# Block sums from kept float32 tiles, and a written order of steps in place of a planner, in a one-core mixer layer

## The chip, the cores and the metric

The kernel runs on one NeuronCore of a Trainium2 chip. The metric is the time on the device, in microseconds (us). Five engines work from queues of their own and wait for each other by semaphores: TensorE (PE; its weight loads have rows of their own, PEld), VectorE (DVE), ScalarE (ACT), GpSimd (POOL), and SyncE (SP), which only issues DMAs.

## The reference

The reference is one pre-norm residual layer for 512 tokens of width 1024, in float32. A combined projection feeds two attention branches of eight heads each: A is latent attention with rotary keys, B keeps the best 128 keys of each query, scored by a small indexer, and adds a relative-position bias. Both are gated and projected, then weighted, summed, projected again, added to the input and normalised.

```python
h = rmsnorm(x, norm_g[l])
(q_lat, c_kv, k_rope, z_a, q_b, k_b, v_b, z_b,
 q_idx, k_idx, w_idx, gate_a, gate_b) = jnp.split(h @ w_in[l], cuts, axis=-1)
...
y_a = mla_attention(q_nope, q_pe, k_nope, k_pe, v_a, pos).reshape(B, S, MLA_WIDTH)
y_a = y_a * jax.nn.silu(z_a)
...
_, idx = lax.top_k(score, topk)
...
y_b = y_b * jax.nn.silu(z_b)
merged = (jax.nn.sigmoid(gate_a) * (y_a @ w_o_a[l])
          + jax.nn.sigmoid(gate_b) * (y_b @ w_o_b[l]))
x = x + merged @ w_out[l]
return rmsnorm(x, final_g)
```

## The kernel before, in words

**Numbers in two parts.** A float32 operand of a matmul is split into a rounded part ("hi", by a cast on ACT) and the remainder ("lo", value minus hi, on DVE or POOL), and a product is three matmuls: hi by hi, lo by hi, hi by lo. The input after normalisation lies transposed in eight tiles of 128 channels by 512 tokens. `normed(k)` (L845) makes tile k in float32 (a tile of class "tmp"), splits it into the pair `hT[k]` (tiles `s_h`), and gives the float32 tile back.

**Products with fewer multiplications.** Some of the projections use block sums: the tokens are halved (columns HI and LO), and the channels too (tile k and tile k+4), and sums and differences of these blocks are multiplied instead of all the blocks. `input_sums()` (L1090) makes these for the four pairs of tiles. For each pair it adds hi and lo again, into two new tiles (`s_tmp<-s_h,s_h`), makes four half-width sums on them in place (`s_tmp<-s_tmp` and `s_tmp<-s_tmp,s_tmp`, 256 columns), and splits the result into hi and lo (`s_hs`). It starts when `SUMS_AT = ("a", 5)` is done, head 5 of branch A. The products that read `s_hs` have sets of 256 columns, and their results meet in tiles `s_pair`, by a copy on ACT (L357) and an addition on DVE (L383).

**Weights.** A load (`raw<-w_...`, by SP, four buffers) is cast on ACT to `s_w` or `s_wo`; the low part is a subtraction on DVE (L383) or POOL (L385). Some weights also have block sums, `s_wsum`.

**Attention.** For each head and each of four tiles of 128 queries, branch A multiplies (L1664 to L1666), takes the row maximum on DVE (`TENSOR_REDUCE`, L1647), and the exponential on ACT. In branch B, ACT first copies the mask of the tile into a PSUM bank (`ps<-mask`, L357), PE adds the products (`ps<-s_op,qhi`), and DVE reads the bank with the bias (L1748). Then the probabilities are scaled by the reciprocal of their sum (`s_p<-s_p,sm`), turned by matmuls with the identity (L481), split (`s_ph`), and multiplied by the values (`ps<-s_ph,vv`).

**What sets the order.** The program is written as some 430 generators ("threads"), each of which yields steps, requests for buffers (`Get`) and conditions (`Until`). `Flow.run` (L224) keeps a model of the free time of each engine and buffer, and picks, each time, the step that would start first by that model. A step that can go to several engines goes where the model sees it end first. On top of the model lie numbers: `SETTLE` asks that PE's operands be ready 2 us before by the model, `NUDGE` adds a drawn number to each thread's rank, `FIRST` picks the second or third candidate at 47 places, `pbias` favours POOL or not, and `PASSED` holds four weight loads back behind 2 or 6 other loads. `Pool_.give` (L136) hands out the free buffer that was used longest ago. The result is one fixed instruction list for each engine. The program does not change it when it runs.

## Time and profile before

| | us |
|---|---|
| median of three runs (420.13 to 420.21) | 420.14 |
| the profiled execution, first to last instruction (its span) | 417.4 |
| PE busy, of the span | 410.4 (98%) |
| DVE busy | 372.8 (89%) |
| ACT busy | 297.9 (71%) |
| POOL busy | 125.7 (30%) |

The span is the profiled execution's own time; the runs are 2.7 us longer, and this part lies outside of the trace. A line of the profile is read so: program line, engine, operation, output tile <- input tiles, the shape, the count; then busy us and the mean in ns of one; then the idle time of that engine before these instructions and what ended it. "PE busy" counts modelled ends of overlapping matmuls, so it does not tell that PE runs at its best pace, only that it is nowhere without work.

### The profile page before, as it was taken

To read this page: it belongs to the slowest core of one execution; us is meant where nothing else is said; L and a number is where in the kernel's file an instruction comes from. 1 tells how busy PE (TensorE), PEld (TensorE's weight loads), DVE (VectorE), ACT (ScalarE), POOL (GpSimd) and SP (SyncE) were. 2 spreads that over 40 slices of the span, in tenths; PEclk is the share of its full clock that TensorE was granted. 3 is DMA by queue.
4 is the path that set the end of the run, shared out by engine and by line. 5 is a ranking of instruction groups with operands and counts; after the bars stand their busy time and mean duration, and the time that the engine had idled before them with its cause. 6 is when DMAs were issued, how large, how long until landed. Compare 5 with 4: busy or idle time off the path is not lost.

```text
span 417.4 us, 7522 instructions
## 1 busy us (share of the span) xinstructions
PE 410.4 (98%) x2494; PEld 370.5 (89%) x2494; DVE 372.8 (89%) x789; ACT 297.9 (71%) x688; POOL 125.7 (30%) x147
## 2 busy tenths in 40 slices
PE   8999999999999999999999999999999999999994
PEld 8999888888888888889999999999998888888883
DVE  4779889569999999999998999799889999999973
ACT  5776888575763846547649978998999975329753
POOL 0037769544464659610000410401001120021330
PEclk9999999999999999999999999999999999999999
DMA  7984135655256351553427336564249767377104
GB/s 266 359 291 143 51 93 190 182 172 136 100 134 188 97 166 40 139 140 110 143 53 204 111 127 175 143 150 149 93 113 296 249 184 240 107 263 264 50 26 176
DMA packets 30790, 65.90 MB, mean 158 GB/s; under 512 B 4792, under 2 KB 6472, under 8 KB 30752
## 3 DMA queue, kind: packets, MB, share of 16 engines
q1 hardware_dynamic: 28400, 61.79, 48.6%
q10 hardware_dynamic: 1584, 2.49, 1.7%
q0 software_dynamic: 768, 1.15, 0.9%
q8 instruction: 19, 0.31, 0.3%
q14 instruction: 19, 0.16, 0.1%
HBM read 50.49 MB, written 4.21 MB: 131 GB/s over the span
## 4 chain that ended last, share of the span: by engine, by line
PE 98%; DVE 0%; ACT 0%; DVEq 0%; issue 0%; ACTq 0%
PE ps L462 88%; PE ps L481 5%; PE ps L1665 1%; PE ps L1666 1%; PE ps L1664 1%; PE ps L957 1%; PE ps L611 1%; DVE s_rg L413 0%; ACT junk L366 0%; PE ps L1008 0%; DVEq L2322 0%; ACT sm L366 0%; DVE sm L2017 0%; DVE zeros L540 0%; DVE neghalf L540 0%
## 5 line engine op out<-in xcount | busy, mean ns | idle before, releaser
L462 PE MATMUL ps<-s_h,s_w 128*128 128x512 f32 (+1 forms) x672 | 135.8, 348 | 0.1
L462 PEld LDWEIGHTS ps<-s_h,s_w 128*128 128x128 f32 x672 | 106.8, 189 | 14.0 <-DVE s_pair L383 0.5
L357 ACT CAST s_w<-raw 128x512 fp32r<-128x512 f32 (+3 forms) x134 | 78.2, 595 | 16.1 <-DVE raw L383 12.1
L385 POOL TENSOR_TENSOR s_w<-raw,s_w 128x512 fp32r<-128x512 f32 (+2 forms) x42 | 52.1, 1253 | 61.5 <-ACT s_w L357 54.1
L383 DVE TENSOR_TENSOR s_w<-raw,s_w 128x512 fp32r<-128x512 f32 (+2 forms) x92 | 59.8, 663 | 9.7 <-ACT s_w L357 9.5
L462 PE MATMUL ps<-s_hs,s_w 128*128 128x256 f32 x384 | 51.9, 285 | 0.0
L462 PEld LDWEIGHTS ps<-s_hs,s_w 128*128 128x128 f32 x384 | 48.3, 191 | 0.1
L462 PE MATMUL ps<-s_ys,s_w 128*128 128x512 f32 x192 | 46.0, 392 | 0.0
L462 PEld LDWEIGHTS ps<-s_ys,s_w 128*128 128x128 f32 x192 | 35.7, 188 | 7.2
L462 PE MATMUL ps<-s_wo,s_mg 128*128 128x512 f32 (+1 forms) x156 | 33.7, 373 | 0.0
L462 PE MATMUL ps<-s_w,s_xg 128*128 128x328 f32 (+1 forms) x192 | 32.5, 323 | 0.0
L462 PEld LDWEIGHTS ps<-s_wo,s_mg 128*128 128x128 f32 x156 | 27.6, 188 | 5.2
L366 ACT ACTIVATE s_p<-s_p,sm 128x256 f32<-128x256 f32 (+3 forms) x58 | 31.0, 548 | 1.4 <-DVE sm L1748 1.3
L462 PEld LDWEIGHTS ps<-s_w,s_xg 128*128 128x128 f32 x192 | 31.4, 188 | 0.0
L357 ACT CAST s_ph<-ps 128x384 fp32r<-128x384 f32 (+1 forms) x48 | 23.6, 517 | 6.7 <-PE ps L481 5.7
L383 DVE TENSOR_TENSOR s_ph<-ps,s_ph 128x384 fp32r<-128x384 f32 (+1 forms) x48 | 27.2, 591 | 1.1 <-ACT s_ph L357 1.1
L366 ACT ACTIVATE s_p<-ps,sm 128x128 f32<-128x128 f32 (+3 forms) x32 | 16.8, 528 | 15.9 <-DVE sm L1647 15.8
L982 DVE MATCH_REPLACE8 mask<-sm,mask 128x384 f32<-128x384 f32 (+2 forms) x48 | 25.9, 542 | 0.0
L981 DVE MAX8 sm<-mask 128x8 f32<-128x384 f32 (+2 forms) x48 | 25.6, 548 | 0.1
L462 PE MATMUL ps<-s_ph,vv 128*128 128x512 f32 (+3 forms) x128 | 25.6, 319 | 0.0
L481 PE MATMUL ps<-ident,s_p 128*128 128x128 f32 x160 | 23.0, 273 | 0.0
L462 PEld LDWEIGHTS ps<-s_ph,vv 128*128 128x128 f32 x128 | 20.6, 189 | 2.0
(206 smaller groups left out, 783.4 us busy)
## 6 DMA issues: line engine op xcount, KB each, us to landing
raw<-w_out SPq DMA_DIRECT2D x18, 512.0 KB, 3.5
s_op<-s_op SPq DMA_DIRECT2D x36, 128.0 KB, 3.4
raw<-w_ga SPq DMA_DIRECT2D x8, 512.0 KB
raw<-w_gb SPq DMA_DIRECT2D x8, 512.0 KB, 3.6
raw<-w_o SPq DMA_DIRECT2D x16, 256.0 KB, 3.6
s_xn<-x SPq DMA_DIRECT2D x8, 256.0 KB, 5.2
bias_scratch<-s_sig ACTq DMA_DIRECT2D x8, 256.0 KB, 2.3
raw<-w_za SPq DMA_DIRECT2D x4, 512.0 KB, 4.5
```

Source lines behind the costliest of these rows:

```text
L357: nc.scalar.copy(dst.ap, src.ap)
L366: nc.scalar.activation(dst.ap, src.ap, func, **kw)
L383: opts.append(("DVE", 0.07 + 0.00104 * x.n, lambda: nc.vector.tensor_tensor(dst.ap, x.ap, y.ap, op=op)))
L385: opts.append(("POOL", 0.15 + 0.0021 * x.n, lambda: nc.gpsimd.tensor_tensor(dst.ap, x.ap, y.ap, op=op)))
L462: nc.tensor.matmul(ps.ap, l.ap, r.ap, start=start and i == 0, stop=stop and i == len(pairs) - 1, skip_group_check=more)
L481: nc.tensor.transpose(d.ap, s.ap, ident.tile)
L611: return lambda: nc.tensor.matmul(ps.tile[:, :n], z[:, :P], z[:, :n], start=True, stop=True)
L957: step = pe(0.005 + n / 2400, [ps.all], [qs[h].all, ks[0].all], lambda: nc.tensor.matmul(ps.tile[:, :n], qs[h].tile[:96, TOK[i]], ks[0].ti ...
L981: yield Step([("DVE", t, lambda: nc.vector.max(m8.tile, work.tile))], [m8], [work])
L982: yield Step([("DVE", t, lambda: nc.vector.match_replace(work.tile, m8.tile, work.tile, MARK))], [work], [m8])
L1664: nc.tensor.matmul(o, q0[0:100], k0[0:100], start=True, stop=False)
L1665: nc.tensor.matmul(o, q0[0:96], k1[0:96], start=False, stop=False)
```

## The change

Two things are changed. First, `normed` takes its float32 tile from a class of its own ("hx") and keeps it, and `input_sums` works on the kept tiles in place: the eight additions hi plus lo are gone, and the eight tiles are held from the normalisation to the sums. The sums may start when head 1 of branch A is done, `("a", 1)`. Second, `Flow.run` no longer decides. It walks a table, `ORDER`, of some 4,000 tokens: each names a thread (its number in base 62), after a dot the choice of engine where there are several, and after an equals sign the buffer that is granted. The model with its numbers is removed, `PASSED` is empty, and three places take their buffers or wait in a way that the table can name.

```diff
-    def give(self, req):
-        if not self.free or (req.cap is not None and self.used.get(req.cls, 0) >= req.cap):
-            return None
-        self.free.sort(key=lambda b: max(b.w, b.r))
-        fits = self.free
-        if req.adds is not None:
-            fits = [b for b in self.free if b.summed[0] <= req.adds[0] and b.summed[1] >= req.adds[1]]
-            if not fits:
-                return None
+    def give(self, req, name):
+        b, = (b for b in self.free if b.name == name)
+        assert req.cap is None or self.used.get(req.cls, 0) < req.cap
+        assert req.adds is None or (b.summed[0] <= req.adds[0] and b.summed[1] >= req.adds[1])
         self.used[req.cls] = self.used.get(req.cls, 0) + 1
-        b = fits[0]
         self.free.remove(b)
...
     def __init__(self):
-        self.free = {"PE": 0.6, "ACT": 0.6, "DVE": 0.6, "POOL": 0.6, "SP": 0.6}
-        self.hw, self.dma, self.adma = 0.6, 0.0, 0.0
-        self.pbias = -1.0
-        self.steps = 0
-        self.port = 0.0
-        self.threads = []
-
...
-    def spawn(self, gen, prio, nudge=None):
-        t = Thread(gen, prio, self.draw.random() * NUDGE if nudge is None else nudge)
+        self.threads, self.made = [], []
+
+    def spawn(self, gen, *rank):
+        t = Thread(gen)
+        self.made.append(t)
...
-    def run(self, stop=None):
-        while self.threads:
-            if stop and stop():
-                return
-            moved = False
-            for t in sorted(self.threads, key=lambda t: t.prio):
-                if isinstance(t.req, Get):
-                    b = t.req.pool.give(t.req)
-                    if b is not None:
-                        self.advance(t, b)
-                        moved = True
-                elif isinstance(t.req, Until) and t.req.cond():
+    def settle(self):
+        again = True
+        while again:
+            again = False
+            for t in list(self.threads):
+                if t.alive and isinstance(t.req, Until) and t.req.cond():
...
+    def run(self):
+        for token in ORDER.split():
+            self.settle()
+            name, _, buf = token.partition("=")
+            name, _, way = name.partition(".")
+            n = 0
+            for c in name:
+                n = 62 * n + DIGITS.index(c)
+            t = self.made[n]
+            step = t.req
+            if buf:
+                self.advance(t, step.pool.give(step, buf))
                 continue
-            best, ready = None, []
-            for t in self.threads:
-                if isinstance(t.req, Step):
-                    for i, (eng, dur, emit) in enumerate(t.req.options):
-                        s = self.start(t.req, eng)
-                        key = ((self.settled(t.req, eng, s) if eng in SETTLE and s < math.inf else s) + BIAS * t.prio + t.nudge, t.prio)
-                    if best is None or mine[5] < best[1][5]:
-                        best = (t, mine)
...
-            turn = FIRST.get(self.steps)
-            self.steps += 1
-            if turn:
-                same = sorted((x for x in ready if x[1][2] == best[1][2]), key=lambda x: x[1][5])
-                best = same[min(turn, len(same) - 1)]
-            t, (_, s, eng, dur, emit, _) = best
-            emit()
...
+            assert all(b.written or b in step.outs for b in step.ins)
+            step.options[int(way or 0)][2]()
             for b in step.outs:
-                b.w = max(b.w, end)
-                b.written, b.by = True, eng
+                b.written = True
...
-
-
-RAW_LAG = {"DVE": 0.125, "POOL": 0.1, "ACT": 0.1}
-BIAS = 0.01
-NUDGE = 0.01
-DRAW = 53
...
+
 PSQUARE = -50
-SETTLE = {'PE': {'DVE': 2.0, 'ACT': 2.0, 'POOL': 2.0, 'SP': 1.0}, 'SP': {'DVE': 1.0, 'ACT': 1.0, 'POOL': 1.0}}
...
-        flow.draw = random.Random(REDRAW)
-        flow.pbias = LATER
...
     def normed(k):
         yield Until(lambda: rbc and k in xg)
-        tmp = yield slot("tmp", TCAP)
+        tmp = yield slot("hx")
         yield stt(tmp.all.f, xt[k].all.f, normg[:, k : k + 1], rbc[0].all.f, ALU.mult, ALU.mult)
         put(xt[k])
         hi = yield slot("h")
         lo = yield slot("h")
         yield act(hi.all, tmp.all.f)
         yield lo_part(lo.all, tmp.all.f, hi.all)
-        put(tmp)
+        hx[k] = tmp
         hT[k] = (hi, lo)
...
     def input_sums():
 
-        yield Until(lambda: sums_due[0] in done)
+        yield Until(lambda: SUMS_AT in done or SUMS_AT is None)
         for k in range(4):
-            f = []
-            for i in (k, k + 4):
-                t = yield slot("tmp", TCAP)
-                yield soon(tt(t.all.f, hT[i][0].all.f, hT[i][1].all.f, ALU.add, BOTH))
-                f.append(t)
+            yield Until(lambda: k in hx and k + 4 in hx)
+            f = [hx[k], hx[k + 4]]
             x, y = (t.all.f for t in f)
             yield soon(tt(x[:, HI], x[:, LO], x[:, HI], ALU.subtract, BOTH))
             yield soon(tt(y[:, HI], y[:, HI], x[:, HI], ALU.subtract, BOTH))
...
         def at(self, i):
-            if self.buf is None:
-                self.buf = yield Get(SMALL)
             c = i - self.group[0]
             return self.buf[:, c : c + 1]
...
     def sums_of_head():
-        return {i: s for s in (Sums(g) for g in GROUPS) for i in s.group}
+        sums = [Sums(g) for g in GROUPS]
+        for s in sums:
+            s.buf = yield Get(SMALL)
+        return {i: s for s in sums for i in s.group}
...
-        ready, sums = set(), sums_of_head()
+        ready, sums = set(), (yield from sums_of_head())
...
         def partial(i):
+            yield Until(lambda: i in seven)
             u3 = seven[i].all.f
...
-ORDER = [0,1,2,3]
+TILES = (0, 1, 2, 3)
...
-FIRST = {
-    283: 2, 456: 1, 606: 1, 1070: 1, 1073: 1, 1078: 1, 1083: 1, 1157: 1, 1297: 1, 1302: 2, 1315: 2, 1328: 1,
...
-PASSED = {7: 2, 8: 2, 9: 2, 10: 6}
-SUMS_AT = ("a", 5)
+PASSED = {}
+SUMS_AT = ("a", 1)
...
+ORDER = (
+    "0=s0 1=s1 2=ps0 6=ps1 6=ps2 6=ps3 6=ps4 6=ps5 6=ps6 0 5=s2 5=s3 3 1 4=s4 4=s5 1 1=s6 1 1=s7 1 1=s8 1 1=s9 1 1=s10 1 1=s11 1 1=raw0 1 1=s12 0 0 0 1 "
...
```

The instructions are, with the exception of the eight additions, the same; their order and engine are not. PE has the same 2,494 matmuls, with the first 176 rows of its queue in the same order and about 1,460 of 2,509 rows in place over the whole. DVE has 721 rows where it had 738, POOL 160 where it had 152. Three places follow. A number behind a name is the tile's or bank's own, and differs between the two programs for the same thing; line numbers differ too.

**At the start of DVE's queue.** `s_er` is the first weight tile as loaded, `s_w_142` its hi part and `s_w_143` the lo part; `s_xg` is the lo part of the first input tile. Before:

```order
L733 TENSOR_SCALAR s_w_142<-s_er_139 128x256
L394 SCALAR_TENSOR_TENSOR s_xg_147<-s_x_140,normg,s_xg_146 128x256
L383 TENSOR_TENSOR s_w_143<-s_er_139,s_w_142 128x256
L394 SCALAR_TENSOR_TENSOR s_xg_147<-s_x_140,normg,s_xg_146 128x128 x2
L383 TENSOR_TENSOR s_w_226<-s_er_149,s_w_225 128x328
L394 SCALAR_TENSOR_TENSOR s_xg_230<-s_x_152,normg,s_xg_229 128x512
```

Now:

```order
L642 TENSOR_SCALAR s_w_142<-s_er_139 128x256
L294 TENSOR_TENSOR s_w_143<-s_er_139,s_w_142 128x256
L305 SCALAR_TENSOR_TENSOR s_xg_147<-s_x_140,normg,s_xg_146 128x256
L305 SCALAR_TENSOR_TENSOR s_xg_147<-s_x_140,normg,s_xg_146 128x128 x2
L294 TENSOR_TENSOR s_w_225<-s_er_149,s_w_224 128x328
L305 SCALAR_TENSOR_TENSOR s_xg_229<-s_x_151,normg,s_xg_228 128x512
```

The lo part of the weight has moved ahead of the 256-column piece of the input's lo part.

**The block sums.** POOL's queue where the first sums are made, before:

```order
L385 TENSOR_TENSOR s_w_1993<-raw_67,s_w_1992 128x512
L385 TENSOR_TENSOR s_tmp_2048<-s_h_615,s_h_616 128x512
L385 TENSOR_TENSOR s_tmp_2052<-s_h_695,s_h_696 128x512
L385 TENSOR_TENSOR s_tmp_2048<-s_tmp_2048 128x256
L385 TENSOR_TENSOR s_tmp_2052<-s_tmp_2052,s_tmp_2048 128x256
L385 TENSOR_TENSOR s_tmp_2048<-s_tmp_2052,s_tmp_2048 128x256
L385 TENSOR_TENSOR s_tmp_2052<-s_tmp_2052 128x256
```

DVE's queue where the second and third pair begin, before:

```order
L383 TENSOR_TENSOR s_hs_2178<-s_tmp_2052,s_hs_2177 128x512
L383 TENSOR_TENSOR s_ph_2096<-ps_99,s_ph_2095 128x512
L981 MAX sm_84<-mask_110 128x8
L982 MATCH_REPLACE mask_110<-sm_84,mask_110 128x256
L383 TENSOR_TENSOR s_tmp_2200<-s_h_681,s_h_682 128x512
L383 TENSOR_TENSOR s_tmp_2217<-s_h_645,s_h_646 128x512
L383 TENSOR_TENSOR s_tmp_2200<-s_tmp_2200 128x256
L383 TENSOR_TENSOR s_y_2232<-ps_95,s_tmp_2226 64x512
L383 TENSOR_TENSOR s_ph_2209<-ps_93,s_ph_2208 128x384
L383 TENSOR_TENSOR s_ph_2214<-ps_98,s_ph_2213 128x384
L981 MAX sm_81<-mask_110 128x8
L383 TENSOR_TENSOR s_tmp_2217<-s_tmp_2217 128x256
```

POOL's queue where the first pair is made, now (`s_hx_518` and `s_hx_522` are the kept float32 tiles):

```order
L296 TENSOR_TENSOR s_hx_518<-s_hx_518 128x256
L296 TENSOR_TENSOR s_w_1440<-raw_68,s_w_1439 128x256
L296 TENSOR_TENSOR s_hx_522<-s_hx_522,s_hx_518 128x256
L296 TENSOR_TENSOR s_y_1407<-s_y_1407,s_z_1188 128x512
L451 MEMSET mask_112 64x64
L296 TENSOR_TENSOR s_hx_518<-s_hx_522,s_hx_518 128x256
L296 TENSOR_TENSOR s_w_1464<-raw_69,s_w_1463 128x512
L296 TENSOR_TENSOR s_w_1503<-raw_69,s_w_1502 128x512
L296 TENSOR_TENSOR s_hs_1497<-s_hx_518,s_hs_1496 128x512
```

And DVE's queue at the same pair, now:

```order
L294 TENSOR_TENSOR s_hx_522<-s_hx_522 128x256
L892 MATCH_REPLACE mask_110<-sm_80,mask_110 128x256
L891 MAX sm_87<-mask_110 128x8
L1551 TENSOR_REDUCE sm_90<-ps_97 128x1
L1551 TENSOR_REDUCE sm_82<-ps_95 128x1
L891 MAX sm_81<-mask_112 128x8
L891 MAX sm_89<-mask_111 128x8
L1551 TENSOR_REDUCE sm_76<-ps_98 128x1
L1551 TENSOR_REDUCE sm_91<-ps_96 128x1
L1551 TENSOR_REDUCE sm_77<-ps_99 128x1
L305 SCALAR_TENSOR_TENSOR s_z_1492<-s_z_1492,ps_94 128x512
L1551 TENSOR_REDUCE sm_78<-ps_92 128x1
```

The additions of two `s_h` are gone, most half-width sums stand in POOL's queue, and the rest stands in DVE's queue between searches for the best keys (`MAX`, `MATCH_REPLACE`) and row maxima of branch A, where before it stood behind nearly all of these.

**ACT's queue in the last heads of branch B.** `ps<-mask` opens a tile of a head; `s_ys` are the hi parts of the gated outputs. Before:

```order
L366 ACTIVATE s_ys_4207<-s_y_2232 128x512
L366 ACTIVATE s_ys_4228<-s_y_4057 128x512
L366 ACTIVATE s_ys_4204<-s_y_1413 128x512
L366 ACTIVATE s_ys_4205<-s_y_1650 128x512
L366 ACTIVATE s_ys_4208<-s_y_3208 128x512
L357 CAST s_w_4172<-raw_67 128x512
L357 COPY ps_97<-mask_110 128x256
L366 ACTIVATE s_p_4115,sm_91<-s_p_4115,sm_85 128x384
L357 COPY ps_99<-mask_112 128x512
L366 ACTIVATE s_p_4181,sm_79<-s_p_4181,sm_89 128x128
L357 COPY ps_92<-mask_111 128x384
L366 ACTIVATE s_p_4202,sm_79<-s_p_4202,sm_82 128x256
```

Now:

```order
L277 ACTIVATE s_ys_4173<-s_y_3186 128x512
L268 COPY s_pair_3965<-ps_94 128x256
L277 ACTIVATE s_ys_4190<-s_y_4070 128x512
L268 CAST s_w_4193<-raw_68 128x512
L268 COPY ps_98<-mask_111 128x384
L268 COPY ps_99<-mask_110 128x256
L268 CAST s_w_4207<-raw_67 128x512
L277 ACTIVATE s_p_4122,sm_88<-s_p_4122,sm_85 128x128
L277 ACTIVATE s_p_4123,sm_88<-s_p_4123,sm_76 128x256
L277 ACTIVATE s_pair_3793<-s_pair_3793 128x512
L277 ACTIVATE s_p_4182,sm_89<-s_p_4182,sm_82 128x128
L268 COPY ps_95<-mask_112 128x512
```

PE's queue where it uses these banks, before (`qhi_72` and `qhi_73` belong to the two heads):

```order
L462 MATMUL ps_93<-s_h_636,s_w_4159 128x512
L462 MATMUL ps_97<-s_op_3236,qhi_73 128x256
L462 MATMUL ps_97<-s_op_3237,qhi_73 128x256
L462 MATMUL ps_93<-s_h_661,s_w_4145 128x512
L462 MATMUL ps_93<-s_h_662,s_w_4145 128x512
L462 MATMUL ps_93<-s_h_661,s_w_4159 128x512
L462 MATMUL ps_99<-s_op_3258,qhi_72 128x512
L462 MATMUL ps_99<-s_op_3384,qhi_72 128x512
L462 MATMUL ps_92<-s_op_3236,qhi_73 128x384
L462 MATMUL ps_92<-s_op_3237,qhi_73 128x384
```

Now:

```order
L373 MATMUL ps_96<-s_h_551,s_w_4194 128x512
L373 MATMUL ps_98<-s_op_3261,qhi_72 128x384
L373 MATMUL ps_98<-s_op_3472,qhi_72 128x384
L373 MATMUL ps_96<-s_h_580,s_w_4193 128x512
L373 MATMUL ps_96<-s_h_581,s_w_4193 128x512
L373 MATMUL ps_96<-s_h_580,s_w_4194 128x512
L373 MATMUL ps_95<-s_op_3261,qhi_72 128x512
L373 MATMUL ps_95<-s_op_3472,qhi_72 128x512
L373 MATMUL ps_96<-s_h_642,s_w_4193 128x512
L373 MATMUL ps_96<-s_h_643,s_w_4193 128x512
L373 MATMUL ps_96<-s_h_642,s_w_4194 128x512
```

Five `s_ys` pieces stood together ahead of three mask copies; now single `s_ys` pieces and casts stand between copies. In PE's queue three tiles of the two heads stood within ten rows; now two tiles of one head stand in eleven.

More of the change, by code (lines that the diff above doesn't have):

```diff
@@ L295, in run @@
             self.advance(t, None)
-RAW_LAG = {"DVE": 0.125, "POOL": 0.1, "ACT": 0.1}
-BIAS = 0.01
-NUDGE = 0.01
-DRAW = 53
+        self.settle()
+        assert not self.threads
 PSQUARE = -50
-SETTLE = {'PE': {'DVE': 2.0, 'ACT': 2.0, 'POOL': 2.0, 'SP': 1.0}, 'SP': {'DVE': 1.0, 'ACT': 1.0, 'POOL': 1.0}}
 TC_ARGS = {}
@@ L971, in scores @@
             put(*qs.values(), *ks)
+            done.add("scored")
         flow.spawn(topk(i), PTOPK)
@@ L1648, in soft @@
                 mx.tile[:, 1:2], ps.tile[:, :n], op=ALU.max, axis=AX.X, negate=True))], [mx], [ps])
-            den = yield from sums[i].at(i)
+            den = sums[i].at(i)
             yield act(probs[i], ps[:, :n], AF.Exp, bias=mx[:, 1:2], scale=1.0, accum=den)
@@ L1653, in soft @@
             ready.add(i)
-        for i in ORDER:
+        for i in TILES:
             nn = P * (i + 1)
@@ L1741, in dsa_head @@
         slots, probs = yield from prob_tiles("p", 6)
-        ready, biased, sums = set(), set(), sums_of_head()
+        ready, biased, sums = set(), set(), (yield from sums_of_head())
         def soft(i, ps):
@@ L1756, in soft @@
                 put(bias)
-            den = yield from sums[i].at(i)
+            den = sums[i].at(i)
             yield act(p, p, AF.Exp, bias=mx[:, 1:2], scale=-1.0, accum=den)
@@ L1762, in soft @@
             ready.add(i)
-        for i in ORDER:
+        for i in TILES:
             nn = P * (i + 1)
```

79 lines of the change are left out of this document (6 added, 73 removed), and 103 rows, old and new, of tables (FIRST, ORDER).

## The prediction

> **What bounds the kernel now.** I read the page first: the busy times and the chain that ended last.
>
> ```profile
> PE 410.4 (98%) x2494; PEld 370.5 (89%) x2494; DVE 372.8 (89%) x789; ACT 297.9 (71%) x688; POOL 125.7 (30%) x147
> ...
> PE 98%; DVE 0%; ACT 0%; DVEq 0%; issue 0%; ACTq 0%
> ```
>
> The chain is PE for 98% of the span. It is not a chain that hops between engines: PE's queue simply runs through. Then I asked for PE's waits. The view of waits (time, number, longest) has one real row for PE, at the start, and a few for its weight loads:
>
> ```profile
> PEld L611 <- DVE neghalf L540: 1.1, 1, 1.1
> PEld ps L462 <- DVE s_pair L383: 0.5, 2, 0.2
> PEld ps L462 <- ACT ps L357: 0.4, 1, 0.4
> ```
>
> The first is the start of the program, which stays. So PE waits for other engines for about 0.9 us after it has begun. The timeline shows where (start, us, engine, what, and in brackets the idle time before):
>
> ```profile
> 260.80 2.20 PEld L462 LDWEIGHTS ps<-s_h,s_w 128*128 128x128 f32 x18 [0.24 <-DVE s_pair L383]
> ...
> 299.81 0.77 PEld L462 LDWEIGHTS ps<-s_h,s_w 128*128 128x128 f32 x6 [0.24 <-DVE s_pair L383]
> ...
> 323.50 0.30 PEld L462 LDWEIGHTS ps<-s_op,qhi 128*128 128x128 f32 x2 [0.44 <-ACT ps L357]
> ```
>
> Whatever the new order does for the other engines, it can give back no more than these three, and a little at the start. What PE itself costs depends on the number of matmuls, which does not change, and on which shapes follow each other. From the chain's pieces in order of time (start, us, what):
>
> ```profile
> 56.73 0.44 PE ps L481 x4
> ...
> 77.71 6.14 PE ps L462 x27
> ```
>
> 27 matmuls of 512 columns take 6.14 us, 0.227 us each; four transposes 0.44 us, 0.11 each although they are 128 columns wide. Going over the pairs of neighbours in both lists of PE with such paces, I find PE's own work the same within 0.1 us (149 transposes follow a transpose before, 145 now). I take 0 for this.
>
> Then the stages, by windows (bounds: length, PE busy, PEld, DVE, ACT, POOL, clock, DMA share, GB/s):
>
> ```profile
> 0.00:100.00 100.00, 98.94 (x556) 89.77 (x557) 76.48 (x149) 73.67 (x169) 51.43 (x72) 1.00 0.61 192
> 100.00:180.00 80.00, 80.00 (x426) 68.63 (x425) 79.45 (x202) 47.87 (x116) 44.88 (x52) 1.00 0.44 122
> 180.00:320.00 140.00, 139.93 (x1077) 135.57 (x1076) 129.87 (x273) 115.20 (x274) 14.12 (x11) 1.00 0.49 138
> 320.00:400.00 80.00, 79.99 (x378) 66.64 (x378) 78.83 (x148) 53.28 (x108) 11.65 (x7) 1.00 0.57 194
> ```
>
> DVE is as full as PE from 100 to 180 us (79.45 of 80) and from 320 to 400 us, and yet PE has no wait there. DVE is behind in the sense that its queue is never empty, but it is ahead of what PE needs. Work taken off DVE is therefore hidden by PE; what counts is whether any single step now comes later than its matmul.
>
> **The change, part by part.**
>
> The sums. The prices by shape (count, busy us, mean ns):
>
> ```profile
> L383 DVE TENSOR_TENSOR s_tmp<-s_h,s_h 128x512 f32<-128x512 f32 x6 | 3.8, 680 | 0.0
> L385 POOL TENSOR_TENSOR s_tmp<-s_h,s_h 128x512 f32<-128x512 f32 x2 | 2.5, 1294 | 0.0
> L383 DVE TENSOR_TENSOR s_tmp<-s_tmp 128x256 f32<-128x256 f32 x5 | 2.1, 414 | 0.0
> L385 POOL TENSOR_TENSOR s_tmp<-s_tmp,s_tmp 128x256 f32<-128x256 f32 x4 | 3.0, 740 | 2.2 <-DVE s_tmp L383 2.0
> L385 POOL TENSOR_TENSOR s_tmp<-s_tmp 128x256 f32<-128x256 f32 x3 | 2.6, 852 | 3.4 <-DVE s_tmp L383 3.4
> L383 DVE TENSOR_TENSOR s_hs<-s_tmp,s_hs 128x512 fp32r<-128x512 f32 x7 | 4.7, 680 | 0.0
> ```
>
> and, from the timeline, the one low part on POOL:
>
> ```profile
> 168.96 1.31 POOL L385 TENSOR_TENSOR s_hs<-s_tmp,s_hs 128x512 fp32r<-128x512 f32 x1
> ```
>
> DVE loses six additions (6 x 0.68 = 4.1 us), six half-width steps that go to POOL (6 x 0.41 = 2.5) and four low parts (4 x 0.68 = 2.7), together 9.3 us. POOL loses two additions (2.6) and takes six half-width steps at about 0.8 (4.8) and four low parts (5.2): 7.4 us more, in a core where POOL is busy for 30%. On PE's path this is worth 0: the first matmul with `s_hs` is at the same place in PE's queue as before, the sums now start some 40 us ahead of it, and PE had no wait for them before. If that cover were gone, one pair of tiles on POOL would cost its chain, 4 x 0.8 + 1.3 = 4.5 us; it is about a tenth of the lead.
>
> The first instructions. The rows around PE's first real work:
>
> ```profile
> 4.18 0.48 DVE L394 SCALAR_TENSOR_TENSOR s_xg<-s_x,normg,s_xg 128x256 fp32r<-128x256 f32 x1 [0.51 <-ACT s_xg L366]
> 4.30 2.16 PE L462 MATMUL ps<-s_xg,s_w 128*128 128x256 f32 x8
> 4.58 0.42 DVE L383 TENSOR_TENSOR s_w<-s_er,s_w 128x256 fp32r<-128x256 f32 x1
> ```
>
> The weight's lo part stands behind a step that waits for ACT until 4.18; it ends at 5.0. In the new order it can run in DVE's idle 0.51 us before, and the step behind is later by at most 0.42. PE runs on through both. Between 0 and 0.42 us could be gained; since PE's row shows no gap that long, I take 0.1.
>
> The three waits. The one at 323.50 has a clear cause in ACT's queue:
>
> ```profile
> 316.55 0.63 ACT L366 ACTIVATE s_ys<-s_y 128x512 fp32r<-128x512 f32 x1
> ...
> 318.04 2.70 ACT L366 ACTIVATE s_ys<-s_y 128x512 fp32r<-128x512 f32 x5
> ...
> 322.98 0.47 ACT L357 COPY ps<-mask 128x384 f32<-128x384 f32 x1
> ```
>
> Five `s_ys` pieces, 2.70 us, stand ahead of the copies of the mask; the last copy ends at 323.45 and PE goes on at 323.50. In the new queue single `s_ys` pieces stand between other steps, and five tiles of the two heads are spread over 54 rows of PE where they stood within 21. To put a number on it: from the matmul that last released ACT to the one that needs the copy, PE had 9.1 us of work before and ACT 9.2 us, a margin of -0.04 us. Now the least margin there is 5.57 - 4.84 = 0.7 us. I take this wait as gone: -0.44. The two waits for `s_pair` have no counterpart at the same place in the new queue, since another product and head stand there: -0.48.
>
> New waits. I took this margin for each step of DVE and ACT that a matmul needs, as an estimate from rows' durations and the two lists. Before, 13 lie under 1.2 us; two of these are under 0.5 and one is 0.51, all three copies of the mask around the wait at 323.50; to the other ten I put the two waits of 0.24, that is 0.048 each. Now 27 lie under 1.2 us (12 of DVE, 15 of ACT), none under 0.5. The table gives up a part of the 2 us that the model kept ready for PE. If each carries what one carried before, the new waits sum to 27 x 0.048 = 1.3 us; if only those above an addition to `s_pair` wait, as in the trace, to 0 to 0.5; if each waited 0.24, to 6.5. I take half of the first, 0.65, since most of the new narrow ones are mask copies and low parts after transposes, kinds that did not wait before with margins of 1.1 to 1.4.
>
> Other steps. POOL takes eleven casts of weights, for which the nearest rows are POOL's one-input step and ACT's cast:
>
> ```profile
> L416 POOL TENSOR_SCALAR s_p<-s_p,sm 128x512 f32<-128x512 f32 x8 | 5.5, 693 | 0.4 <-DVE sm L1614 0.3
> L357 ACT CAST s_w<-raw 128x512 fp32r<-128x512 f32 x110 | 67.0, 620 | 13.7 <-DVE raw L383 12.1 <-issue 0.4 <-ACT s_sig L366 0.4
> ```
>
> That is 0.07 us later per cast (0.69 against 0.62), and at worst 0.7 more if rounding doubles it; the loads lie several us ahead of their matmuls. In exchange POOL gives up sixteen scalings of 0.4 to 0.7 us, three of `s_latraw` among them. 0 for these. `PASSED` moves four weight loads on SP's queue between 36 and 46 us; the first 32 loads stand as before, and no wait of PE names a DMA: 0. The early request of small buffers and `partial`'s wait only fix an order that the table fixes anyway: 0. The end, from the last matmul to the last output, has the same steps in the same order:
>
> ```profile
> 411.65 0.38 ACT L366 ACTIVATE junk<-ps 128x256 f32<-128x256 f32 x1 [1.00 <-PE ps L462]
> ...
> 413.28 0.35 ACTq L2030 DMA_DIRECT2D out<-s_rg  x1
> ```
>
> The sum: -0.44 - 0.48 - 0.1 + 0.65 = -0.4 us. The profiled execution's span would go from 417.4 to 417.0; the runs' median is 2.7 us above the span, outside it, so 420.14 becomes 419.8. A measurement here can tell a change of about 0.2% (0.84 us) from none, so this is no change.
>
> **The ports.** DVE's and POOL's steps sometimes hold each other up, as a row shows:
>
> ```profile
> L383 DVE TENSOR_TENSOR s_tmp<-s_tmp,s_tmp 128x512 f32<-128x512 f32 x2 | 2.7, 1368 | 0.0
> ```
>
> A step of this shape takes 0.68 alone, and here 1.37, so 0.69 us is the price of one meeting. POOL has eight rows more than before: if each met one such step, DVE would lose 5.5 us, against 9.3 us that it gets rid of. That would matter only where it falls on one narrow margin. (The Trainium skill, "SBUF — State Buffer", section "Who interferes with whom", says that a VectorE step with two SBUF inputs contends with a GpSimd step that reads SBUF, and that the loser waits for the whole instruction. The 1.37 agrees with this; by the rule alone, the moved sums speak against the change, and the sum would rise by what is a rival below.)
>
> **The rivals.**
>
> *All waits go (faster).* The new margins are all above 0.5 us and none binds. For it: before, ACT steps with margins of 1.1 did not wait. Against it: two additions did, at these margins or a little above. Then -0.44 - 0.48 - 0.1 to -0.3 at the start: 419.0.
>
> *The head start is spent (slower).* The place is the turnaround of bank and operand in attention and paired products: PE finishes a tile, DVE or ACT handles it, PE needs it some 12 matmuls later. The price is the trace's 0.24 us, and it decides as soon as a margin under 1.2 us waits as a rule and not in one case of five. With the twelve of DVE: 12 x 0.24 = 2.9, less the 1.0 that goes: 422.0. For it: 27 margins against 13. Against it: most of the old ones cost nothing.
>
> *POOL holds DVE back (slower).* Two or three meetings of 0.69 us each fall on margins of 0.5 to 0.9 at 100 to 150 us, where the sums now run between DVE's row maxima, and PE loses about 0.6 at each of three: 420.14 - 0.4 + 1.8 = 421.5. Against it: DVE's rows with a PSUM input keep their time while POOL is busy.
>
> *The kept tiles crowd out weights (slower).* Eight tiles stay held for some 70 us longer. A load that is late by its whole landing time would cost 3.5 us by the row below; for a load that is late by half, 421.9. Against it: no wait for a DMA, and DMA queues half idle.
>
> ```profile
> raw<-w_out SPq DMA_DIRECT2D x18, 512.0 KB, 3.5
> ```
>
> **How the numbers follow.** The forecast of no change has a chance of 0.48 and its own range of 419.3 to 421.0. All waits gone: 0.26. The head start spent: 0.16. POOL holds DVE back: 0.06. Crowded tiles: 0.04. So faster is 0.26, same 0.48, slower 0.26. Eight times in ten the time should lie between 418.9, just under the case of no waits, and 421.7, short of the worst of the slower cases.
>
> **What would show it.** PE's waits and those of its weight loads after: the row `ACT ps L357` (by its new line) should be gone, and new rows for DVE and ACT of 0.1 to 0.3 us each should sum to about 0.65. PE's busy time should stay within 0.5 us, DVE's fall by some 9 to 11 us, POOL's rise by about as much as 8. The additions `s_tmp<-s_h,s_h` should be gone, and no row of a wait for `s_hs` should appear. The prediction is wrong if PE's busy time moves by over 0.5 us with the same matmuls, if the waits sum to over 2 us, or if a matmul waits for a DMA.

## The result and the profile after

The changed kernel takes 423.97 us in the median of its runs (423.31 to 424.31) against 420.16 (420.13 to 420.21): a ratio of 1.0095, 95% interval 1.008 to 1.0109. It is slower by 3.8 us. The forecast of no change was wrong, and so was the range, which ended at 421.7.

The page of the changed kernel, busy times and chain:

```profile
PE 411.5 (98%) x2494; PEld 370.1 (88%) x2494; DVE 373.5 (89%) x773; ACT 296.7 (70%) x688; POOL 141.2 (33%) x155
...
PE 79%; DVE 13%; DMA 3%; ACT 2%; issue 2%; SPq 1%; DVEq 0%; ACTq 0%
```

Two things stand out. DVE has 16 instructions fewer than before (773 against 789) and is busy for 0.7 us more (373.5 against 372.8). And the chain, PE for 98% before, runs through DVE for 13%. The waits of the weight loads (time, number, longest):

```profile
PEld ps L373 <- DVE s_wo L294: 2.0, 2, 1.0
PEld ps L373 <- ACT s_pair L268: 1.8, 1, 1.8
...
PEld ps L373 <- DVE ps L305: 0.9, 1, 0.9
PEld ps L915 <- DVE s_lat L305: 0.7, 2, 0.4
PEld ps L1570 <- DMA s_op<-s_qpe: 0.5, 1, 0.5
```

and where the long ones lie:

```profile
201.26 1.85 PEld L373 LDWEIGHTS ps<-s_hs,s_w 128*128 128x128 f32 x15 [1.76 <-ACT s_pair L268]
...
397.68 10.72 PEld L373 LDWEIGHTS ps<-s_wo,s_mg 128*128 128x128 f32 x59 [0.95 <-DVE s_wo L294]
409.35 0.77 PEld L373 LDWEIGHTS ps<-s_wo,qhi 128*128 128x128 f32 x4 [0.94 <-DVE ps L305]
411.14 4.77 PEld L373 LDWEIGHTS ps<-s_wo,qhi 128*128 128x128 f32 x32 [1.03 <-DVE s_wo L294]
```

With three rows of 0.2 us that are not shown, waits for other engines and DMAs sum to 6.5 us, against 0.9 before. The rows of PE itself have 3.5 us of them (1.6, 1.1, 0.5 and 0.3), and PE's busy time is 1.1 us longer; together that is the 4.6 us by which the span grew (417.4 to 422.0). The medians differ by 3.8, since what lies outside the span varied (2.7 us for the execution shown of before, 1.8 here). The loss is no crowd of small waits: four long ones, one at 201 us and three at the end, have 4.7 of the 6.5 us, and DVE made the last three. The end of the chain that ended last is DVE's too: from 382.77 to 411.10 us all its pieces are DVE's, but for 2.0 us in which the profile shows nothing that was waited for.

```profile
382.77 1.25 DVE s_wsum L294
...
410.49 0.61 DVE s_wo L294
...
411.15 4.98 PE ps L373 x32
```

The stages, in the columns of the prediction:

```profile
0.00:100.00 100.00, 98.95 (x559) 89.50 (x560) 78.71 (x157) 73.75 (x171) 37.28 (x56) 1.00 0.62 191
100.00:180.00 80.00, 79.66 (x421) 67.95 (x420) 77.94 (x185) 56.70 (x137) 47.70 (x51) 1.00 0.41 113
180.00:320.00 140.00, 138.44 (x1068) 134.23 (x1067) 125.56 (x264) 105.61 (x250) 35.26 (x29) 1.00 0.49 142
320.00:400.00 80.00, 79.47 (x371) 66.06 (x370) 74.59 (x137) 51.16 (x106) 15.50 (x14) 1.00 0.58 197
400.00:422.00 22.00, 15.00 (x83) 12.35 (x81) 16.72 (x34) 9.45 (x27) 5.51 (x7) 0.92 0.26 96
```

and the last stage of the kernel before:

```profile
400.00:417.40 17.40, 11.55 (x64) 9.85 (x62) 8.18 (x21) 7.90 (x23) 3.66 (x7) 0.95 0.33 121
```

Between 100 and 400 us DVE is idle for 2.06 + 14.44 + 5.41 = 21.9 us; before it was 0.55 + 10.13 + 1.17 = 11.9. Summed from the end, DVE has as much left at 180 us as before (216.9 us in both), 4.3 us more at 320 us, and 8.5 us more at 400 us (16.72 against 8.18). PE itself has 3.4 us more left at 400 us (15.00 against 11.55), so some 5 of the 8.5 us are a lag of DVE behind PE; the rest is common to both. The 9.3 us of steps taken off DVE would have paid for the 10 us of idling, had the busy time fallen with them. Why it did not shows in the group of low parts of weights. Before (count, busy us, mean ns, idle):

```profile
L383 DVE TENSOR_TENSOR s_w<-raw,s_w 128x512 fp32r<-128x512 f32 x78 | 52.9, 687 | 7.5 <-ACT s_w L357 7.2
```

After:

```profile
L294 DVE TENSOR_TENSOR s_w<-raw,s_w 128x512 fp32r<-128x512 f32 x77 | 58.2, 765 | 3.9 <-ACT s_w L268 2.5 <-POOL s_w L337 0.8
```

The same step takes 78 ns more in the mean: 6.0 us over 77 steps, while POOL is busy for 15.5 us more (141.2 against 125.7). I call it a meeting when a step of DVE and one of POOL overlap and one of them lasts longer for it. Taking for each shape of DVE's steps the shorter quarter's duration as its time alone, and counting those that last over 0.15 us longer, I find 16 long steps with 8.6 us of excess before and 26 with about 16 us after; all 26 stand beside a step of POOL. Six of the 16 and three of the 26 read a PSUM bank, and steps of that kind last so in both kernels; without them it is 10 steps with 7.2 us and 23 with 15.3. What a meeting looks like, from the timeline of the changed kernel (start, us, engine):

```profile
396.94 1.29 DVE L294 TENSOR_TENSOR s_wo<-s_wsum,s_wo 128x512 fp32r<-128x512 f32 x2
398.15 1.78 DVE L294 TENSOR_TENSOR s_wsum<-raw,s_wsum 128x512 f32<-128x512 f32 x1
...
397.64 1.74 POOL L296 TENSOR_TENSOR s_wo<-raw,s_wo 128x512 fp32r<-128x512 f32 x1 [4.63 <-DVE s_wo L294]
```

POOL's step starts while DVE's pair of steps runs, and lasts 0.45 us longer than its 1.29 alone. Then DVE's next step, which takes 0.68 alone, starts while POOL's still runs and lasts 1.78; it ends 0.55 us after POOL's end at 399.38. Each waits for most of the other's step. The Trainium skill, "SBUF — State Buffer", section "Who interferes with whom", states that the engine that issues first holds the port pair that both share for its whole instruction and the other blocks. This trace agrees, with the numbers above.

At 201 us the chain of waits, read in order of time, shows the other place of the loss:

```profile
185.80 12.49 PE ps L373 x72
198.29 0.67 DVE raw L294
198.96 0.61 DVE s_w L294
...
199.60 0.70 DVE raw L294
...
200.32 0.63 ACT s_w L268
...
201.03 0.20 ACT s_pair L268
```

PE needs ACT's copy to `s_pair`. It stands in ACT's queue behind two casts of weights, and each cast waits for a sum in `raw` that DVE makes late:

```profile
198.99 0.62 ACT L268 CAST s_w<-raw 128x512 fp32r<-128x512 f32 x1 [1.75 <-DVE raw L294]
...
200.32 0.62 ACT L268 CAST s_w<-raw 128x512 fp32r<-128x512 f32 x1 [0.71 <-DVE raw L294]
```

A meeting stands ahead of these sums in DVE's queue:

```profile
193.23 1.30 POOL L296 TENSOR_TENSOR s_w<-raw,s_w 128x512 fp32r<-128x512 f32 x1 [0.73 <-ACT s_w L268]
193.41 1.67 DVE L294 TENSOR_TENSOR s_w<-raw,s_w 128x512 fp32r<-128x512 f32 x1
```

### The profile page after: what moved, and what is told of

It reads as the page before. It is cut to its first block, busy times and chain, and to the rows that moved or that the text cites. A ratio compares the mean times of both kernels' runs of the same rounds, so it can differ in the third digit from the quotient of the medians.

```text
span 422.0 us, 7534 instructions
## 1 busy us (share of the span) xinstructions
PE 411.5 (98%) x2494; PEld 370.1 (88%) x2494; DVE 373.5 (89%) x773; ACT 296.7 (70%) x688; POOL 141.2 (33%) x155
## 4 chain that ended last, share of the span: by engine, by line
PE 79%; DVE 13%; DMA 3%; ACT 2%; issue 2%; SPq 1%; DVEq 0%; ACTq 0%
PE ps L373 71%; PE ps L392 4%; DVE s_wsum L294 1%; DVE mask L892 1%; DVE sm L891 1%; DMA s_op<-s_qpe 1%; DVE s_wo L294 1%; DMA raw<-w_out 1%; SPq L417 1%; DVE s_xr L305 1%; PE ps L520 1%; DMA s_op<-s_op 1%; DVE mask L305 1%; PE ps L1570 1%; PE ps L1569 1%
## 5 line engine op out<-in xcount | busy, mean ns | idle before, releaser
L373 PE MATMUL ps<-s_h,s_w 128*128 128x512 f32 (+1 forms) x672 | 139.9, 349 | 0.0
L268 ACT CAST s_w<-raw 128x512 fp32r<-128x512 f32 (+3 forms) x126 | 72.3, 592 | 23.4 <-DVE raw L294 15.5
L296 POOL TENSOR_TENSOR s_w<-raw,s_w 128x512 fp32r<-128x512 f32 (+3 forms) x41 | 52.4, 1284 | 79.5 <-ACT s_w L268 58.8
L294 DVE TENSOR_TENSOR s_w<-raw,s_w 128x512 fp32r<-128x512 f32 (+3 forms) x93 | 67.8, 740 | 5.9 <-ACT s_w L268 4.5
L373 PE MATMUL ps<-s_hs,s_w 128*128 128x256 f32 x384 | 53.4, 285 | 1.6 <-ACT s_pair L268 1.6
L373 PEld LDWEIGHTS ps<-s_hs,s_w 128*128 128x128 f32 x384 | 49.6, 191 | 2.4 <-ACT s_pair L268 1.8
L373 PE MATMUL ps<-s_ys,s_w 128*128 128x512 f32 x192 | 46.9, 392 | 0.0
L277 ACT ACTIVATE s_p<-s_p,sm 128x512 f32<-128x512 f32 (+3 forms) x66 | 35.0, 546 | 2.0 <-DVE sm L1515 1.3
L373 PE MATMUL ps<-s_ph,vv 128*128 128x512 f32 (+3 forms) x128 | 27.2, 319 | 0.0
```

Source lines behind the costliest of these rows:

```text
L268: nc.scalar.copy(dst.ap, src.ap)
L277: nc.scalar.activation(dst.ap, src.ap, func, **kw)
L294: opts.append(("DVE", 0.07 + 0.00104 * x.n, lambda: nc.vector.tensor_tensor(dst.ap, x.ap, y.ap, op=op)))
L296: opts.append(("POOL", 0.15 + 0.0021 * x.n, lambda: nc.gpsimd.tensor_tensor(dst.ap, x.ap, y.ap, op=op)))
L373: nc.tensor.matmul(ps.ap, l.ap, r.ap, start=start and i == 0, stop=stop and i == len(pairs) - 1, skip_group_check=more)
```

## The experiments

**Theory M** (meetings): the new order sets POOL's reads beside DVE's two-input steps, DVE's saving is lost, and its lag makes PE wait. **Rivals**: the amount of DVE's work in this order (W), ACT's queue, POOL's own lateness (E). Other letters in the expectations: A and A1 put the loss down to the order and not to the sums, and O to the order of DVE's queue alone; D says that DVE is the bound from 380 us on whatever PE waited for before, P that PE's waits add up. All ratios are against the kernel before.

**1. The order without the additions' removal, and the reverse.** First, the order before with the eight additions left out and nothing else moved (the sums take the high tiles instead of the additions' results, so the low parts of the input are left out of them):

```diff
-  yield soon(tt(t.all.f, hT[i][0].all.f, hT[i][1].all.f, ALU.add, BOTH))
-  yield soon(tt(x[:, HI], x[:, LO], x[:, HI], ALU.subtract, BOTH))
+  u, v = (hT[i][0].all.f for i in (k, k + 4))
+  yield soon(tt(x[:, HI], u[:, LO], u[:, HI], ALU.subtract, BOTH))
```

> The old order, written out as a table that gives the same instruction lists as the kernel before, without the eight additions. The half-width sums read the hi parts directly, so the low parts of the input are left out of the block sums; everything else is computed. Theory A (what went wrong is the new order and choice of engines, not the sums): DVE and POOL lose 6 and 2 additions at 150 to 190 us, where PE never waits for them, so 420.1 to 420.3, no change. Rival B (the shorter sums in themselves shift DVE and POOL against each other so that they meet more often): 421 to 424.

Measured: 419.86 us, ratio 0.9998 (0.9987 to 1.0009). Second, the new order with the eight additions put back on DVE:

```diff
+            for i in (k, k + 4):
+                yield tt(hx[i].all.f, hT[i][0].all.f, hT[i][1].all.f, ALU.add)
```

> The changed kernel with the eight additions put back, on DVE, in place on the kept tiles, directly ahead of each pair's sums (5.4 us more work for DVE between 108 and 150 us). Theory A1 (DVE as a whole is late in the changed kernel; what it is given early it hands on to the end): 427 to 429, with longer waits of PE for DVE after 380 us. Rival (DVE's idle time between 200 and 380 us takes the additions up): 424.0 within 0.5.

Measured: 429.64 us, ratio 1.0239 (1.0218 to 1.026), 6 us above the new order. The additions as a group (count, busy us, mean ns, idle):

```profile
L294 DVE TENSOR_TENSOR s_hx<-s_h,s_h 128x512 f32<-128x512 f32 x8 | 5.1, 680 | 0.0
```

The first of its new waits, from the timeline of the weight loads:

```profile
118.23 0.19 PEld L1570 LDWEIGHTS ps<-s_op,qhi 100*128 100x128 f32 x1 [1.35 <-DVE s_z L305]
```

More of them follow up to 170 us; the waits at the end, where theory A1 had put the cost, stay as they were. So 5 us of DVE's steps are worth nothing in the old order and cost 6 us in the new one, slightly more than expected. The old order had room on DVE's side for them; the new one, where they stand, has none. This is no exact reverse: all eight are on DVE here, at the places of the new sums, where before two were on POOL and six stood elsewhere in DVE's queue. It does not tell their amount from their places.

**2. POOL's reads taken away.** In both orders POOL's low parts become a subtraction of one column and a fill of the rest, which reads nothing (these low parts are left out):

```diff
-        return tt(lo, x, hi.f, ALU.subtract, ("DVE",) if in_ps(x) else engs)
+            def emit():
+                nc.gpsimd.tensor_tensor(lo.ap[:, :1], x.ap[:, :1], hi.f.ap[:, :1], op=ALU.subtract)
+                nc.gpsimd.memset(lo.f.ap[:, 1:], 0.0)
```

> The changed kernel, with each low part that POOL makes cut to one column of subtraction, the rest of the tile written as zeros by POOL. It leaves these low parts out of the products; the order, the engines and the waits on inputs stay. POOL then reads SBUF only for a moment in these steps. Theory M (meetings of DVE and POOL: 26 long DVE steps, 16 us in the changed kernel, 17 steps and 9 us before): most long DVE steps are gone, DVE ends early, the wait at 201 us falls from 1.6 to 0.6 us and the three at 397 to 411 us vanish: 420.0 to 420.8. Rival O (the order of DVE's queue alone, its 9 us of new idle time after 100 us): the three waits at the end stay at over 2 us, 422.5 to 424.

> The same cut of POOL's low parts in the old order (these low parts are left out of the products). PE is the bound there and has no wait that a meeting causes: both theories expect 419.9 to 420.3. If it comes out below 419.7, meetings cost the kernel before something as well.

Measured: the new order 420.66, ratio 1.002 (1.001 to 1.0031); the old order 419.89, ratio 1.0003 (0.9991 to 1.0015). What costs nothing in the old order costs 0.75%, 3.2 us, in the new one. But POOL also has less to do here, and its results come earlier. So a third kernel fills twice, and POOL's steps last about as long as before:

```diff
-                nc.gpsimd.memset(lo.f.ap[:, 1:], 0.0)
+                for _ in range(2):
+                    nc.gpsimd.memset(lo.f.ap[:, 1:], 0.0)
```

> The changed kernel with POOL's low parts cut to one column as in the run with short low parts, but the zeros are written twice, so that each step of POOL lasts about as long as in the changed kernel (0.24 + 2 x 0.52 = 1.3 us) and weight buffers come free as late as there. The low parts that POOL makes are left out of the products. Theory M (what cost the time is that POOL's reads hold up DVE): 420.3 to 421.0, as with the short ones. Rival E (the short steps helped because POOL was done earlier and loads started earlier): 422.5 to 424.

Measured: 420.43, ratio 1.0016 (1.0002 to 1.0029). Its page:

```profile
PE 410.6 (98%) x2494; PEld 369.7 (88%) x2494; DVE 363.8 (87%) x773; ACT 296.5 (71%) x688; POOL 133.6 (32%) x271
```

The group (count, busy us, mean ns, idle):

```profile
L294 DVE TENSOR_TENSOR s_w<-raw,s_w 128x512 fp32r<-128x512 f32 x77 | 53.9, 710 | 3.7 <-ACT s_w L268 2.5 <-POOL s_w L337 0.8
```

And the timeline at the place of the meeting shown above:

```profile
396.22 0.70 DVE L294 TENSOR_TENSOR s_wsum<-raw,s_wsum 128x512 f32<-128x512 f32 x1
...
396.31 1.11 POOL L362 MEMSET s_wo<- 128x511 f32 x2
```

The low parts of weights are back at 710 ns, and the very step that took 1.78 us beside POOL's subtraction takes 0.70 beside its fills. POOL is busy for 133.6 us, not much less than the 141.2 of the changed kernel. DVE's busy time falls by 9.7 us. Not all of this is new with the change: in the old order the single fill takes 3.7 us off DVE (372.8 to 369.1), and there it is worth nothing:

```profile
PE 410.4 (98%) x2494; PEld 369.8 (89%) x2494; DVE 369.1 (88%) x789; ACT 298.1 (71%) x688; POOL 94.3 (23%) x199
```

So meetings with POOL's low parts cost DVE some 6 us more in the new order than in the old. It is the reading that costs, not POOL's time. Theory M holds for 0.8% of the 0.95%.

**3. The two places.** At the end, only the two low parts at 397.64 and 403.21 are filled (and left out):

```diff
-        if len(step.options) > 1 and len(lo.ap.shape) == 2:
+        if len(step.options) > 1 and len(lo.ap.shape) == 2 and lo.buf.tile.name.startswith(("s47_wo836", "s73_wo839")):
```

> The changed kernel with only two of POOL's low parts, those that met DVE at 398.1 and 403.4 us (1.10 us each), without a long read in the same way; their low parts are left out. Theory M: DVE is the bound at the end, so 2 x 1.1 = 2.2 us come off, 421.8, as far as PE does not become the bound first (not under 421.0). Rival (many small delays over the whole program, the last two do not matter alone): over 423.0.

Measured: 422.11, ratio 1.0052 (1.0036 to 1.0068), 1.8 us below the new order; the waits at 409 and 411 are gone. At 201 us, the kernel with two fills already has a shorter wait, 0.79 us where the changed kernel has 1.76, about as much less as the 1.0 us of the meeting at 193.41:

```profile
199.78 1.85 PEld L382 LDWEIGHTS ps<-s_hs,s_w 128*128 128x128 f32 x15 [0.79 <-ACT s_pair L268]
```

In the changed kernel, ACT's copy now goes ahead of the casts:

```diff
+L268 COPY s_pair_2419<-ps_99 128x256
 L268 CAST s_w_2470<-raw_66 128x512
 L268 CAST s_w_2498<-raw_69 128x512
-L268 COPY s_pair_2419<-ps_99 128x256
```

> The changed kernel with one step of ACT moved: the copy to s_pair that PE waits for at 201 us stands ahead of the two casts that wait for DVE. Theory D (DVE is the bound from 380 us on, whatever PE waited for before): PE is 1.6 us earlier after 201 us and waits that much longer near the end; 423.3 to 424.2. Rival P (PE's waits add up): 422.3.

Measured: 422.81, ratio 1.0068 (1.0042 to 1.0093), 1.1 us below, between the numbers of D and P, so that neither is confirmed. The wait of 1.76 us is gone, and two of 0.2 to 0.3 us follow it. The copy's place is a part of its own: DVE is the reason why the casts are late, but the copy needs neither cast. Both edits together, POOL's low parts as one column and two fills everywhere (left out, as above) and the copy ahead:

> The run with POOL's low parts as one column and two fills (these low parts are left out), and in it ACT's copy to s_pair ahead of the cast. It asks whether the two parts found so far are the whole loss. Theory M with the copy: 420.43 less the wait of 0.79 us at 199.8, so 419.5 to 420.0, which is the time of the kernel before to within what can be told. If a third part is left, the time stays at or above 420.3.

Measured: 419.92, ratio 0.9991 (0.998 to 1.0002): the whole loss is gone, in a kernel that leaves low parts out. Leaving them out is in itself worth nothing in the old order (1.0003). Its page:

```profile
PE 410.2 (98%) x2494; PEld 369.6 (89%) x2494; DVE 363.4 (87%) x773; ACT 296.7 (71%) x688; POOL 133.4 (32%) x271
```

Its stages between 100 and 400 us, by windows:

```profile
100.00:180.00 80.00, 80.00 (x423) 68.29 (x422) 78.21 (x187) 56.43 (x136) 45.73 (x99) 1.00 0.41 114
180.00:320.00 140.00, 139.74 (x1075) 135.45 (x1074) 123.60 (x268) 107.96 (x256) 31.17 (x52) 1.00 0.50 148
320.00:400.00 80.00, 80.00 (x380) 66.77 (x379) 74.58 (x137) 51.29 (x104) 16.82 (x33) 1.00 0.55 187
```

DVE still idles between 100 and 400 us for 1.79 + 16.40 + 5.42 = 23.6 us, no less than in the changed kernel. This idling belongs to the new order and costs nothing here, where DVE's busy time is 10 us lower; and the old order's meetings cost nothing there. The loss is the two together.

**4. Eleven casts back to ACT.** POOL's one-input casts return to ACT, at the same places in the table.

```diff
-L337 TENSOR_SCALAR s_w<-raw 128x512      (POOL)
+L268 CAST s_w<-raw 128x512               (ACT)
```

> The changed kernel with the eleven casts of weights on POOL sent back to ACT, in the same places of the order (ACT 6.8 us more of its 30% idle time; POOL 11 reads fewer, seven of which stand in the list of long DVE steps, 2 us in all). Theory M with D: 1 to 2 us come off, 422 to 423. Rival (ACT's queue gets late where its copies are narrow): 424 to 426.

Measured: 426.83, ratio 1.0172 (1.0141 to 1.0203), 3.2 us above the new order: theory M's number was missed, and the time is above the rival's 424 to 426 too. DVE's busy time fell (371.1), and 20 long steps are left of 26, so meetings did go; but DVE waits more for ACT. The waits of DVE, here:

```profile
DVE s_w L294 <- ACT s_w L268: 12.8, 14, 2.9
```

and in the changed kernel:

```profile
DVE s_w L294 <- ACT s_w L268: 8.3, 12, 1.6
```

DVE's low parts wait 4.5 us longer in sum for ACT's casts. The rival with ACT's queue was nearer: here DVE seems to lose more in waiting than it gains from fewer meetings.

**5. Steps given to DVE instead.** If a meeting costs DVE 1.0 us and the step itself 0.68, DVE should do the step, by theory M. Three versions: the two low parts at the end; thirteen steps from 193 us on; and the thirteen with the copy moved.

```diff
-L296 TENSOR_TENSOR s_wo_4976<-raw_69,s_wo_4975 128x512        (POOL)
-L296 TENSOR_TENSOR s_wo_4994<-s_wsum_4394,s_wo_4993 128x512   (POOL)
+L294 TENSOR_TENSOR s_wo_4976<-raw_69,s_wo_4975 128x512        (DVE)
+L294 TENSOR_TENSOR s_wo_4994<-s_wsum_4394,s_wo_4993 128x512   (DVE)
```

> The new order with only the two low parts of the output weights at 397.64 and 403.21 given to DVE instead of POOL; everything is computed. Leaving the two out saved 1.8 us. Theory M: each delay of about 1.1 us goes and 0.68 comes back on DVE: 0.8 us of DVE's lag less at the end, so 422.6 to 423.4. Rival W: two steps more on the engine that sets the end, 1.4 us later: 425 to 426.

> The new order with thirteen of POOL's two-input steps from 193 us on given to DVE: those that stood beside a lengthened DVE step or were lengthened themselves in the trace after the change (for example the low part at 199.69, 1.73 us, and the two at 397.64 and 403.21). Everything is computed. DVE gets 13 x 0.68 = 8.8 us of steps more. Theory M (a POOL step that reads SBUF makes a two-input DVE step about 1.0 us longer, and DVE's lag at 201 and at the end is made of that): up to 13 such delays go, 13 us, so DVE's busy time is 369 to 373 in spite of the added steps, the waits at 397 to 411 shrink, and the time is 421.5 to 423. Rival W (DVE is late because of the amount of its steps in this order, as the eight added additions suggest, where 5.4 us of steps cost about 6 us): DVE's busy time rises by 6 us or more, and the time is 427 to 432.

> The same thirteen steps on DVE, and ACT's copy to s_pair ahead of the cast that waits for DVE's sum, as in the run that moved it alone. Theory M with the copy as a part of its own: 1.1 us below the run with the thirteen steps alone, so 420.4 to 422. If DVE, with more to do at 195 to 201, makes the cast later still, the copy alone saves more than 1.1 here. Rival W: 426 to 431.

Measured: 425.87, ratio 1.0136 (1.0116 to 1.0156); 427.76, ratio 1.019 (1.0158 to 1.0223); 427.82, ratio 1.0182 (1.0165 to 1.0199). All three missed theory M's numbers and came out where rival W had put them. Two rows of the two-step version explain it in part:

```profile
407.10 0.68 DVE L294 TENSOR_TENSOR s_wo<-s_wsum,s_wo 128x512 fp32r<-128x512 f32 x1
...
407.83 4.41 PEld L373 LDWEIGHTS ps<-s_wo,s_mg 128*128 128x128 f32 x14 [2.97 <-DVE s_wo L294]
```

PE waits 2.97 us for just this low part. On POOL it was done at 404.7; at the same place of the table, in DVE's queue, it stands behind ten steps that DVE starts after the cast has ended (at 401.66). So this edit tested the step's place. In the run with thirteen steps, DVE's busy time rose by 4.7 us (to 378.2) for 8.8 us of steps: by the difference, at most 4.1 us came back from meetings, not the 13 that I had set against them. With the copy moved as well, nothing is gained: the wait of 2.0 us for `s_pair` goes, but those for `s_wo` grow from 3.0 to 3.9 us and those for mask copies from 0.4 to 1.3. So taking meetings away does not help where it gives DVE as much work in their place.

To part place from amount, the second low part and its cast were moved up in the table, to before the additions of `s_xr`, once with both low parts on DVE and once with both left on POOL:

```diff
 L294 TENSOR_TENSOR s_wo_4996<-s_wsum_4260,s_wo_4995 128x512
+L294 TENSOR_TENSOR s_wo_4994<-s_wsum_4394,s_wo_4993 128x512
 L294 TENSOR_TENSOR s_xr_4837<-s_xr_4837,s_part_4885 128x512
```

> The new order with the two low parts of the output weights on DVE, as in the run that gave them to DVE at the end (425.87), but the second of them does not stand at its old place in the table, where DVE came to it at 407.10 with PE waiting since 404.86: it and ACT's cast ahead of it are moved up, to before the three additions of s_xr at 402.84. Everything is computed. Theory M with the place: the 2.97 us wait came from the step's place in DVE's queue; two delays of 1.1 us go, 2 x 0.68 come back, so 422.6 to 423.6 (0.5 to 1.5 us below the new order). Rival W (the amount of DVE's steps at the end decides, wherever they stand): 1.4 us above the new order, 425 to 426.

> The control for it: the same two moves in the table (ACT's cast and the low part up, before the additions of s_xr), with both low parts left on POOL. Everything is computed. Theory M: POOL's step still stands beside DVE's, only some 1 us earlier, and a two-input step of DVE is still made 1.0 us longer: within 0.6 us of the new order, 423.5 to 424.6. If the early cast were what helps, it would fall as far as the other run, to 422.6 to 423.6.

Measured: 423.12, ratio 1.008 (1.0064 to 1.0097), and 423.56, ratio 1.0079 (1.0065 to 1.0094). Both lie 0.6 us below the new order, too little for the intervals to tell it from none, and by ratio they do not differ. So the 1.7 us of the earlier version came from the step's place, not from the amount of two steps: rival W's 425 to 426 is ruled out for these two. But doing the two on DVE is no gain over meeting them. Theory M had set the two runs apart; each median still lies in its range, but what is gained can come from the earlier place alone, as the control's other expectation says. The rows of the version on DVE show why:

```profile
401.19 1.46 DVE L294 TENSOR_TENSOR s_wo<-raw,s_wo 128x512 fp32r<-128x512 f32 x1
...
400.80 1.30 POOL L296 TENSOR_TENSOR s_xr<-s_xr,s_part 128x512 f32<-128x512 f32 x1 [6.56 <-issue]
```

The low part itself now meets POOL's next step and takes 1.46. Two delays of 1.1 us went (2.2), and 0.68 + 1.46 = 2.1 came.

## Why the prediction was wrong, by its own steps

*The sums, "on PE's path this is worth 0".* True in the old order (ratio 0.9998). In the new one, eight additions put back cost 6 us. I had priced the step against the old order's slack and not against that of the new.

*"Work taken off DVE is therefore hidden by PE".* This is the step that failed, together with "The ports", which gave the sum no term. It needs DVE's lead, the time by which its results come before PE needs them, to stay as it was. In the new order DVE idles 10 us more between 100 and 400 us, so the 9.3 us of saving were needed, and meetings took them: DVE's busy time did not fall by 9 to 11 us but rose by 0.7. My price of one meeting, 0.69 us, fits the mean of the 23 (15.3 us, 0.67 each) by luck: the row that I took it from is two steps of 0.84 and 1.90 us. The meetings ahead of the long waits, at 193.41, 398.15 and 403.44, cost 1.0 to 1.1 us each. I had allowed for eight more, 5.5 us, and found 13 more, 8.1 us. So the size was too small, but near. What was wrong was the judgement that followed: "that would matter only where it falls on one narrow margin". The delays add up along DVE's queue, and the sum arrives where DVE has to be on time: with POOL's long reads replaced by fills, 0.8% of the 0.95% is gone.

*The rival "POOL holds DVE back"*, with a chance of 0.06, named the mechanism. Its place was wrong: not three margins at 100 to 150 us, but 201 us and the end; its 421.5 was 2.5 us short. *"The head start is spent"* had the right idea of a lead used up, but looked for it in twelve waits of 0.24 us. Of *the kept tiles* nothing shows: no matmul waits for a weight load.

*"New waits", 0.65 us.* Measured: 6.5 us with the loads' small ones. The margins were worked out with each step's time alone and each queue on its own, so a lag that builds up from 180 to 400 us could not appear in them. Four waits, not 27, carry 4.7 us of it.

*"The end, from the last matmul to the last output"* at 0. This held: it takes 5.9 us in both kernels (411.55 to 417.4, and 416.12 to 422.0). The 2.9 us of waits lie just ahead of it, in the last products, to which DVE comes some 5 us behind PE; for these the sum had nothing but "New waits".

*"The eleven casts" at 0.* In this order they are better on POOL: back on ACT they cost 3.2 us. No run tests the other half of the exchange, the sixteen scalings.

*What held.* The three waits of before are gone, at 260.8, 299.8 and 323.5, with only 0.17 us at 288 for a copy of the mask; the additions `s_tmp<-s_h,s_h` are gone; no matmul waits for `s_hs`.

*The signs of being wrong.* All three came: the waits sum to over 2 us, a load waits 0.5 us for a DMA (`s_op<-s_qpe`, at 136.64), and PE's busy time moved by 1.1 us, more than the 0.5 allowed. With the same queue PE's busy time is 410.6 and 410.2 in the two kernels with two fills, but 411.2 in the one with a single fill, so that PE's own work is unchanged is likely and not shown. POOL's busy time rose by 15.5 us, where I had said about 8.

*What stays open.* The planner of before kept the two apart by a rule: its `start` returns the later of the step's time and `self.port` where `shares` says that the step uses the port, a DVE step whose inputs lie in SBUF or a reading POOL step. That the table has no such rule agrees with 16 long steps before and 26 after; no order with that rule and the new sums was built, so that this rule makes the difference is argued, not shown. Which of the new order's neighbours cause DVE's 10 us of idling is not settled either. No kernel here beats the one before: the nearest equal it, and in the new order only with low parts left out.
